# Turned queries read from PSUM, mLSTM heads at one step of the DeltaNet units, their loads and outputs issued by GpSimd, and earlier reads of the mLSTM output

## The chip, the cores and the metric

The kernel runs on one core of a Trainium2 chip. A core has TensorE (matrix products into PSUM), VectorE, ScalarE and GpSimd (elementwise work), SyncE (SP, which here only issues DMAs), and sixteen DMA engines that move data between the chip's memory and the on-chip memory SBUF. Each engine takes its instructions in order; semaphores order the engines among each other. DMAs are issued from the queues of SP, ScalarE and GpSimd.

The metric is the device time of one execution in microseconds (us). Lower is better.

## The reference

One decoder layer on 512 tokens of width 2048, with two token mixers side by side, an mLSTM with 8 heads (q and k of width 128, v of width 256) and a gated DeltaNet with 16 heads of width 128. Everything is float32.

```python
u = _rmsnorm(h, norm_w)
proj = jnp.matmul(u, w_in)            # q, k, v, o, z, gates of both mixers, two merge gates
h_a = _mlstm_chunkwise(heads(ml_q), heads(ml_k), heads(ml_v), i_pre, logf)   # q is scaled by dk ** -0.5
h_a = _merge_heads(_rmsnorm(h_a)) * ml_norm_w * sigmoid(ml_o) * silu(ml_z)
qkv = _causal_conv_silu(dn_qkv, dn_conv_w)
h_b = _gated_delta_chunkwise(l2norm(dq), l2norm(dk_), dv_, beta, g)
h_b = _merge_heads(_rmsnorm(h_b, dn_norm_w)) * silu(dn_z)
y = sigmoid(gate_a) * (h_a @ w_out[:ML_WIDTH]) + sigmoid(gate_b) * (h_b @ w_out[ML_WIDTH:])
out = _rmsnorm(x + y, final_norm_w)
```

In the mLSTM, q and k meet only in products of one with the other (the scores, and q times a state that is built of k and v). The factor dk ** -0.5 may therefore stand on either.

## The kernel before

Every large product is done in float32 accuracy out of three products of rounded parts: an operand x is cast to a high part `hi` and the rest `lo = x - hi`, and hi·hi, hi·lo and lo·hi are added up in PSUM. `split_hi` (L139, ScalarE) and `split_lo` (L142, VectorE) make the parts of the weights, some steps before TensorE needs them. `uh` and `ul` hold the parts of the activations.

The program runs in these stages:

1. Load and normalise x, turn it into `uh`, `ul`; project the first query and key heads.
2. `seven_stage`: the projections z, s, q, v and the merge gates. Each block multiplies two column groups c1 and c2 by a scheme of seven products for eight (`m6`, `m1`, `m5`, `m7`, sums in `U1` and `C22`). What ends a block is a "sink": it takes the results out of PSUM and writes them to memory. The q block (`sink_q`) takes the queries and keys of mLSTM heads 4 to 7. They are needed with the channel on the partitions: `V.transpose` turns blocks of 32x32, and four DMAs of 64 KB each (32 partitions, 16 blocks, runs of 128 bytes) put the blocks in place in `qt_d`; the keys are also written unturned to `k_d`.
3. `dn_unit`, eight units (L1105 and on). A unit projects K, V and Q of two DeltaNet heads (`proj_cm`, 16 steps each), and beside the matmuls the convolution, the norms, the solver of the delta rule and the chains of both heads run (`dn_front_k`, `dn_front_q`, `dn_back`, `dn_chain`). The eight mLSTM heads (`ml_head`) run beside the units too: loads of q, k, v, the scores `psc` (L1169), four chunks of products `pnum` and `pcs`, the gates `mg`, a turn, and the write to `hm_d`.
4. `load_h` reads `hm_d` back and splits it into `uh`, `ul` for the first part of the output projection (`wide_block`, three column blocks). Then `h_d`, the DeltaNet output, is read back, and `seven_stage` runs again with `w_out`.
5. `load_hm` reads `hm_d` a second time for the last column block (`last_block`), where the final norm and the output follow.

The order of the work: TensorE runs in the order in which the program is written. The program counts steps (`tick()`), one for every six matmuls or so; a generator that `start(gen, wait)` registers is continued at its due step, and `yield n` puts it off by n steps. A unit is 48 steps. The other engines' order is made by a planner that simulates the engines before the kernel is built: an instruction goes where it is ready, by priority. `urgent(...)` raises a priority, and `behind("A")`, `behind("V")`, `behind("S")` place an instruction right behind the newest weight cast of ScalarE, the newest weight difference of VectorE or the newest weight read of SP. On the chip the order of each queue is then fixed.

Tiles come from rings with a fixed number of buffers under a tag: "wr" has four, "tg" three, "to" two (turned tiles on their way out), "g" two (`gz` and `mg`); "mkq", "mkw", "mw" and "mv1" have one each (q and k, k turned back, decays, v). A buffer is free when all that reads it is done, a DMA included.

Lines that the prediction speaks of: L738 and L744, the turn and the four DMAs of `sink_q`; L853 and L863, the turn and the write of `turn`; L811, row broadcasts; L902, `pk`, the first product of a unit's solver, which needs the convolved key `kq` (L837); L1002, the first product of `dn_back`; L1082, the load of `gz`; L1098 and L1099, the norm factor of a chain's end and its product with `gz` on GpSimd; L1102, VectorE's product that waits for it; L1143, L1151, L1179 and L1213, the head's loads; L1157, the decays of a head; L1245 and L1246, the splits of `load_h` and `load_hm`; L1394, L1448 and L1565, other DMAs of GpSimd; L1520, the reads of `load_hm`.

Of the kernel before, what the change touches and what calls it, by code (L numbers as in the profile page):

```python
# [45 lines left out]

UNITS = list(range(8))
QKS = 2 * QKFIRST * P

# [8 lines left out]
def hybrid_body(  # L58
# [671 lines left out]
    def sink_q(c1, c2, m1, m5, m7, last):  # L730

        def turned(x_, c, a):
            if a:
                with behind("A"):
                    nc.scalar.dma_start(k_d[c], x_)
            o = spare(True)
            with behind("V"):
                V.transpose(o, x_)  # L738
            to = qt_d[a * 4:(a + 1) * 4].rearrange("h (j r) (n a c) -> r (h j) n a c", r=BS, n=NC, c=BS)
            ov = o.rearrange("p (m c) -> p m c", c=BS)  # L740
            for b in range(4):
                yield 1
                with behind("A"):
                    nc.scalar.dma_start(to[:, :, c, b, :], ov[b * BS:(b + 1) * BS])  # L744

        def out_(ps, t, a, wait):
            z = spare(False)
            with urgent(3):
                A.mul(z, ps, (float(P) ** -0.5, 1.0)[a])
            start(turned(z, t, a), wait + 6 * t)  # L750

        def end5(t):
            add(m5[t], U1[t], m5[t])
            out_(m5[t], t, 1, 8)

        def late_q(t):
            with behind("A"):
                A.mul(U1[t], U1[t], float(P) ** -0.5)
            yield from turned(U1[t], 2 + t, 0)

        def end7(t):
            add(U1[t], U1[t], m7[t])
            start(turned(C22[t], 2 + t, 1), 14 + 6 * t)
            start(late_q(t), 17 + 6 * t)

        return (lambda t: out_(m1[t], t, 0, 4)), end5, end7

# [80 lines left out]

    def turn(src, dst, out=False, lag=5):


        o = dst if dst is not src and len(dst.shape) == 3 else wk.tile([P, NC, P], F32, tag="to", name="to", bufs=2)
        V.transpose(o if len(src.shape) == 3 else o.rearrange("p n c -> p (n c)"), src)  # L853
        start(travel(o, dst, out, lag > 3), lag if out else 2)

    def travel(o, dst, out, apart):

        d = dst if len(dst.shape) == 4 else dr.tile([16, BS, 4, BS], F32, tag="td", name="td", bufs=8)
        ov = o.rearrange("p n (j c) -> p (n j) c", c=BS)
        if out:  # L860
            for a in range(4):
                with behind("A"):
                    nc.scalar.dma_start(d[:, :, a, :].rearrange("m r c -> r m c"), ov[a * BS:(a + 1) * BS])  # L863
# [178 lines left out]
    def dn_chain(j, hs, kq, u, soon):  # L1042
# [7 lines left out]
        for c in range(NC):  # L1050
# [29 lines left out]
            if c == 1:  # L1080
                g = wk.tile([P, NC, P], F32, tag="g", name="gz", bufs=2)
                nc.sync.dma_start(g, gz_d[:, :, h * P:(h + 1) * P].rearrange("c p n -> p c n"))  # L1082
            if c < NC - 1:
# [17 lines left out]
        with urgent():  # L1101
            V.tensor_tensor(out=g, in0=po, in1=g, op=ALU.mult)  # L1102
        turn(g, h_d[h], True, 5 if h < 2 * UNITS[-1] else 3)

# [33 lines left out]
    def ml_head(h):  # L1138
# [49 lines left out]
        for c in range(NC):  # L1188
# [20 lines left out]
            if c == NC - 2:  # L1209
                g = [wk.tile([P, NC, P], F32, tag="g", name="mg", bufs=2) for _ in range(2)]  # L1210
                for i in range(2):
                    col = h * NB + i * P
                    nc.sync.dma_start(g[i], g_d[:, :, col:col + P].rearrange("c p n -> p c n"))  # L1213
            yield 3
# [33 lines left out]
    def load_h():  # L1248

        raws_ = []  # L1250

        def load():
            if len(raws_) < KH:
                if len(raws_) % 2:
                    r = wkb.tile([P, NC, NB + 1], F32, tag="mv1", name="hr", bufs=1)
                    r = r.rearrange("p c n -> p (c n)")[:, 0:2 * S].rearrange("p (a s) -> p a s", s=S)
                else:
                    r = wkb.tile([P, 2, S], F32, tag="mkq", name="hr", bufs=1)
                for n in range(2):
                    load_tile(r[:, n, :], hm_d[2 * len(raws_) + n])  # L1260
# [12 lines left out]

    for h in range(MLH):
        start(ml_head(h), 1 + 42 * h, "B")
    start(open_y(), 200)
# [261 lines left out]
    def sink_last(c1, c2, m1, m5, m7):  # L1538
# [3 lines left out]
        def half_b():  # L1542
# [191 lines left out]
```

## Time and profile before

| | us |
|---|---|
| runs | 2216.82, 2210.53, 2212.88 |
| median | 2212.88 |
| profiled execution | 2213.26 |
| its span, first to last instruction | 2211.5 |
| mean granted clock of TensorE in it | 0.993 |

A profile is of one execution. Its lines name the engine (PE TensorE, PEld its weight loads, DVE VectorE, ACT ScalarE, POOL GpSimd, SP SyncE; a "q" behind it is the engine's queue, which issues DMAs and waits), the line of the kernel, and the tiles as out<-in. In a list of waits the figures are us in all, number of times, longest; the name behind the arrow is what ended the wait. In a view by stretches each row has start and end in us from the beginning of the span, then the busy time of each engine with its number of instructions, the granted clock of TensorE (1.00 is full speed), the busy share of the DMA engines, and GB/s. Matmuls overlap in the profile, so a busy TensorE isn't one at its peak.

### The profile page before, as it was taken

How to read it: one execution, taken by the hardware profiler on the slowest of the kernel's cores; microseconds unless marked ns; L12 is line 12 of the kernel's file. 1: busy time of each engine (PE TensorE's matmuls, PEld its weight loads, DVE VectorE, ACT ScalarE, POOL GpSimd, SP SyncE). 2: the span in 40 equal slices, each digit the busy share in tenths (PEclk: the TensorE clock that was granted, in tenths of full speed). 3: DMA queues.
4: the chain of work that ended last, by engine and by line, in shares of the span. 5: the costliest groups of instructions: out<-in, count | busy, mean ns of one | idle time of the engine just before them, and what ended most of it. 6: DMA issues, size and time to landing. Idle time of an engine off the chain costs nothing.

```text
span 2211.5 us, 31646 instructions
## 1 busy us (share of the span) xinstructions
PE 2146.4 (97%) x10544; PEld 1761.4 (80%) x10544; DVE 1698.6 (77%) x2937; ACT 1035.6 (47%) x1996; POOL 291.4 (13%) x395
## 2 busy tenths in 40 slices
PE   6999999999999999999999999999999999999997
PEld 5877777878887888888888888887877887877785
DVE  5787788788878777777857788778778776578886
ACT  5444444444444444444445545545445464344345
POOL 0320000000000000000012422324314121110200
PEclk9999999999999999999999999999999999999998
DMA  5456676667668757776867677768768577687886
GB/s 157 122 180 189 196 215 191 213 195 231 201 217 240 232 186 231 233 223 189 262 203 176 168 186 183 180 153 208 175 160 213 141 189 193 186 261 212 242 281 222
DMA packets 532006, 444.20 MB, mean 201 GB/s; under 512 B 250369, under 2 KB 385762, under 8 KB 531714
## 3 DMA queue, kind: packets, MB, share of 16 engines
q1 hardware_dynamic: 400946, 350.33, 55.2%
q10 hardware_dynamic: 124192, 74.02, 10.9%
q0 software_dynamic: 6704, 17.83, 3.6%
q8 instruction: 82, 1.34, 0.3%
q14 instruction: 82, 0.67, 0.1%
HBM read 348.66 MB, written 97.58 MB: 202 GB/s over the span
## 4 chain that ended last, share of the span: by engine, by line
PE 65%; DMA 14%; DVE 10%; issue 4%; ACT 2%; SPq 2%; POOL 1%; ACTq 0%; DVEq 0%; POOLq 0%
PE ps L577 11%; PE ps L578 11%; PE ps L576 10%; PE pj L256 8%; PE pj L257 8%; PE pj L258 8%; DVE wl L142 4%; DMA wr<-t_d 3%; DMA wr<-in_w_in_dram 2%; ACT wh L139 2%; DMA wr<-in_w_out_dram 1%; SPq L504 1%; DVE t L518 1%; DMA hr<-h_d 1%; PE py L1369 1%
## 5 line engine op out<-in xcount | busy, mean ns | idle before, releaser
L139 ACT CAST wh<-wr 128x512 fp32r<-128x512 f32 (+1 forms) x522 | 373.1, 717 | 388.8 <-PE pj L257 189.9
L142 DVE TENSOR_TENSOR wl<-wr,wh 128x512 fp32r<-128x512 f32 (+1 forms) x522 | 442.3, 850 | 144.1 <-ACT wh L139 137.1
L256 PE MATMUL pj<-uh,wh 128*128 128x512 f32 x896 | 373.6, 417 | 1.8 <-ACT yp L821 1.8
L258 PE MATMUL pj<-uh,wl 128*128 128x512 f32 x896 | 351.3, 392 | 0.0
L257 PE MATMUL pj<-ul,wh 128*128 128x512 f32 x896 | 350.9, 392 | 0.0
L577 PE MATMUL ps<-wl,uh 128*128 128x512 f32 x752 | 296.8, 395 | 5.7 <-DVE wl L142 5.1
L576 PE MATMUL ps<-wh,uh 128*128 128x512 f32 x752 | 294.7, 392 | 2.7 <-DVE X L630 2.4
L578 PE MATMUL ps<-wh,ul 128*128 128x512 f32 x752 | 294.0, 391 | 0.0
L139 ACT CAST wh<-ts 128x512 fp32r<-128x512 f32 x240 | 148.2, 617 | 256.4 <-DVE ts L536 209.6
L139 ACT CAST wh<-t 128x1024 fp32r<-128x1024 f32 x120 | 126.3, 1052 | 270.1 <-PE ps L578 144.1
L577 PE MATMUL ps<-wl,suh 128*128 128x512 f32 x624 | 243.1, 390 | 4.1 <-DVE wl L142 4.1
L576 PE MATMUL ps<-wh,suh 128*128 128x512 f32 x624 | 243.5, 390 | 1.0 <-ACT wh L139 0.5
L578 PE MATMUL ps<-wh,sul 128*128 128x512 f32 x624 | 242.9, 389 | 0.0
L258 PEld LDWEIGHTS pj<-uh,wl 128*128 128x128 f32 x896 | 168.7, 188 | 37.2
L256 PEld LDWEIGHTS pj<-uh,wh 128*128 128x128 f32 x896 | 169.5, 189 | 32.3 <-ACT yp L821 2.3
L257 PEld LDWEIGHTS pj<-ul,wh 128*128 128x128 f32 x896 | 169.6, 189 | 28.2
L142 DVE TENSOR_TENSOR wl<-ts,wh 128x512 fp32r<-128x512 f32 x240 | 164.4, 688 | 35.2 <-ACT wh L139 35.2
L142 DVE TENSOR_TENSOR wl<-t,wh 128x1024 fp32r<-128x1024 f32 x120 | 147.4, 1228 | 52.6 <-ACT wh L139 51.9
L577 PEld LDWEIGHTS ps<-wl,uh 128*128 128x128 f32 x752 | 141.8, 189 | 44.2 <-DVE wl L142 15.7
L576 PEld LDWEIGHTS ps<-wh,uh 128*128 128x128 f32 x752 | 141.7, 188 | 36.1 <-DVE X L630 6.3
L578 PEld LDWEIGHTS ps<-wh,ul 128*128 128x128 f32 x752 | 141.9, 189 | 28.7
L536 DVE TENSOR_TENSOR ts<-wr 128x512 f32<-128x512 f32 x120 | 82.8, 690 | 100.1 <-DMA wr<-t_d 77.8
(319 smaller groups left out, 3587.6 us busy)
## 6 DMA issues: line engine op xcount, KB each, us to landing
wr<-in_w_in_dram SPq DMA_DIRECT2D x744, 256.0 KB, 3.7
wr<-in_w_out_dram SPq DMA_DIRECT2D x138, 256.0 KB, 4.7
t_d<-ts ACTq DMA_DIRECT2D x104, 256.0 KB, 4.0
wr<-t_d SPq DMA_DIRECT2D x104, 256.0 KB, 3.9
xt<-in_x_dram SPq DMA_DIRECT2D x8, 512.0 KB, 7.4
tg_d<-X ACTq DMA_DIRECT2D x16, 256.0 KB, 5.6
tg_d<-to ACTq DMA_DIRECT2D x16, 256.0 KB, 6.0
v<-v_d SPq DMA_DIRECT2D x8, 512.0 KB, 5.2
```

The costliest lines, as they stand in the source:

```text
L139: newest["A"] = A.copy(hi, src).ins
L142: newest["V"] = V.tensor_tensor(out=lo, in0=src, in1=hi.bitcast(F32), op=ALU.subtract).ins
L256: T.matmul(ps[j], hi[:, k, wsl], uh[:, kt, :], start=(kt == 0), stop=False)
L257: T.matmul(ps[j], hi[:, k, wsl], ul[:, kt, :], start=False, stop=False)
L258: T.matmul(ps[j], lo[:, k, wsl], uh[:, kt, :], start=False, stop=(kt == KT - 1))
L504: newest["S"] = nc.sync.dma_start(to, src).ins
L518: V.tensor_tensor(out=t13, in0=r[:, 1:3, :], in1=r[:, 0:2, :], op=ALU.subtract)
L536: V.tensor_tensor(out=ts[:, 0, :], in0=r[:, 0, :], in1=r[:, 2, :], op=ALU.subtract)
L576: T.matmul(ps[t], ah, hi, start=(g == "A" and i == 0), stop=False, skip_group_check=True)
L577: T.matmul(ps[t], ah, lo, start=False, stop=False, skip_group_check=True)
L578: T.matmul(ps[t], al, hi, start=False, stop=(i == KH - 1), skip_group_check=True)
L1369: T.matmul(ps[c], uh[:, kt, tsl], hi, start=(kt == ks[0]), stop=False)
```

## The change

It has four parts.

- **Query block.** `end1` turns the first two query blocks straight from PSUM on VectorE. The scale is put on the keys instead of the queries (ScalarE, four times instead of six). The turned tiles come from "wr" instead of "tg", the 32 writes to `qt_d` are issued by GpSimd, two a step, and the waits of the pieces are set anew.
- **Heads.** The starts of the mLSTM heads are a list, `HEADS`, in place of 1 + 42h; from head 3 on they are 48 steps apart.
- **Issuers.** GpSimd issues the writes to `hm_d` (ScalarE before) and the loads of q, k, v, `mg` and of DeltaNet's `gz` (SP before).
- **Reading ahead.** `load_h` holds three pairs of tiles instead of two (the third in "mkw" and "mw"), and its splits are placed behind the weights'. `load_hm` reads four tiles ahead instead of two, into two rings, "hmr" and "hs", and starts two steps earlier.

```diff
+HEADS = (1, 41, 85, 130, 178, 226, 274, 322)
...
     def sink_q(c1, c2, m1, m5, m7, last):
 
-        def turned(x_, c, a):
+        def place(o, c, a):
+            to = qt_d[a * 4:(a + 1) * 4].rearrange("h (j r) (n a c) -> r (h j) n a c", r=BS, n=NC, c=BS)
+            ov = o.rearrange("p (m c) -> p m c", c=BS)
+            for b in range(4):
+                G.dma_start(to[:, :, c, b, :], ov[b * BS:(b + 1) * BS])
+                if b % 2:
+                    yield 1
+
+        def turned(x_, c, a, scale):
+            if scale:
+                with behind("A"):
+                    A.mul(x_, x_, float(P) ** -0.5)
             if a:
                 with behind("A"):
                     nc.scalar.dma_start(k_d[c], x_)
-            o = spare(True)
+            o = spare(False)
             with behind("V"):
                 V.transpose(o, x_)
...
+            yield 1
+            yield from place(o, c, a)
+
+        def end1(t):
+            o = spare(False)
+            with urgent(3):
+                V.transpose(o, m1[t])
+            start(place(o, t, 0), 2 + 3 * t)
...
         def end5(t):
             add(m5[t], U1[t], m5[t])
...
             z = spare(False)
             with urgent(3):
-                A.mul(z, ps, (float(P) ** -0.5, 1.0)[a])
-            start(turned(z, t, a), wait + 6 * t)
+                A.mul(z, m5[t], float(P) ** -0.5)
+            start(turned(z, t, 1, False), 10 + 4 * t)
...
         def end7(t):
             add(U1[t], U1[t], m7[t])
-            start(turned(C22[t], 2 + t, 1), 14 + 6 * t)
-            start(late_q(t), 17 + 6 * t)
+            start(turned(U1[t], 2 + t, 0, False), 16 + 3 * t)
+            start(turned(C22[t], 2 + t, 1, True), 22 + 4 * t)
...
-                nc.sync.dma_start(g, gz_d[:, :, h * P:(h + 1) * P].rearrange("c p n -> p c n"))
+                G.dma_start(g, gz_d[:, :, h * P:(h + 1) * P].rearrange("c p n -> p c n"))
...
-        turn(g, h_d[h], True, 5 if h < 2 * UNITS[-1] else 3)
+        turn(g, h_d[h], nc.scalar, 5 if h < 2 * UNITS[-1] else 3)
...
-            nc.sync.dma_start(kq[:, 1 - i, :], (qk_d if first else qt_d)[2 * QKFIRST * i + h % (2 * QKFIRST)])
+            G.dma_start(kq[:, 1 - i, :], (qk_d if first else qt_d)[2 * QKFIRST * i + h % (2 * QKFIRST)])
...
-            with behind("S"):
-                nc.sync.dma_start(kw, k_d[:, :, h * P - QKS:(h + 1) * P - QKS].rearrange("c p n -> p c n"))
+            with behind("V"):
+                G.dma_start(kw, k_d[:, :, h * P - QKS:(h + 1) * P - QKS].rearrange("c p n -> p c n"))
...
-        nc.sync.dma_start(v1[:, :, 0:NB], v_d[:, :, h * NB:(h + 1) * NB].rearrange("c p n -> p c n"))
+        G.dma_start(v1[:, :, 0:NB], v_d[:, :, h * NB:(h + 1) * NB].rearrange("c p n -> p c n"))
...
-                    nc.sync.dma_start(g[i], g_d[:, :, col:col + P].rearrange("c p n -> p c n"))
+                    G.dma_start(g[i], g_d[:, :, col:col + P].rearrange("c p n -> p c n"))
...
-            turn(g[i], hm_d[2 * h + i], True)
+            turn(g[i], hm_d[2 * h + i], G)
...
+                m = len(raws_) % 3
+                if m == 2:
...
+                elif m:
+                    r = [wkb.tile([P, NC, P], F32, tag=t, name="hr", bufs=1).rearrange("p c n -> p (c n)") for t in ("mkw", "mw")]
...
-        load()
-        load()
-        yield 4
+        for _ in range(3):
+            load()
+            yield 1
+        yield 1
...
-                split_scaled(uh[:, k, :], ul[:, k, :], raws_[i][:, n, :], normc[:, 16 + k:17 + k])
+                with behind("A"), behind("V"):
+                    split_scaled(uh[:, k, :], ul[:, k, :], raws_[i][n], normc[:, 16 + k:17 + k])
...
-        start(ml_head(h), 1 + 42 * h, "B")
+        start(ml_head(h), HEADS[h], "B")
...
-            r = fin["pool"].tile([P, NO], F32, tag="hmr", name="hmr", bufs=3)
+            if len(raws_) % 2:
+                r = late["sb"].tile([P, NO], F32, tag="hs", name="hmr", bufs=4)
+            else:
+                r = fin["pool"].tile([P, NO], F32, tag="hmr", name="hmr", bufs=3)
...
-        for _ in range(2):
-            load(nc.sync)
-        yield 4
+        for _ in range(4):
+            with behind("S"):
+                load(nc.sync)
+            yield 1
...
-            start(load_hm(), 5)
+            start(load_hm(), 3)
```

More of the change, by code (lines that the diff above doesn't have):

```diff
@@ L735, in turned, with end5 @@
                     nc.scalar.dma_start(k_d[c], x_)
-            o = spare(True)
+            o = spare(False)
             with behind("V"):
                 V.transpose(o, x_)
[L739 to L746, printed above, removed]
+            yield 1
[5 more added lines that the diff above has]
+            start(place(o, t, 0), 2 + 3 * t)
+        def end5(t):
+            add(m5[t], U1[t], m5[t])
             z = spare(False)
             with urgent(3):
-                A.mul(z, ps, (float(P) ** -0.5, 1.0)[a])
-            start(turned(z, t, a), wait + 6 * t)
[L752 to L759, printed above, removed]
+                A.mul(z, m5[t], float(P) ** -0.5)
+            start(turned(z, t, 1, False), 10 + 4 * t)
         def end7(t):
             add(U1[t], U1[t], m7[t])
-            start(turned(C22[t], 2 + t, 1), 14 + 6 * t)
-            start(late_q(t), 17 + 6 * t)
-        return (lambda t: out_(m1[t], t, 0, 4)), end5, end7
+            start(turned(U1[t], 2 + t, 0, False), 16 + 3 * t)
+            start(turned(C22[t], 2 + t, 1, True), 22 + 4 * t)
+        return end1, end5, end7
     SINK = {"q": sink_q, "g": sink_flat(lambda c, col: tg_d[c, :, col - GATE:col - GATE + NO], AF.Tanh, 0.5),
@@ L847, in token_norms, with turn @@
                 A.activation(jk, pk[:, c, :], AF.Square, accum_out=dst[:, c:c + 1])
-    def turn(src, dst, out=False, lag=5):
+    def turn(src, dst, out=None, lag=5):
         o = dst if dst is not src and len(dst.shape) == 3 else wk.tile([P, NC, P], F32, tag="to", name="to", bufs=2)
@@ L861, in travel @@
             for a in range(4):
-                with behind("A"):
-                    nc.scalar.dma_start(d[:, :, a, :].rearrange("m r c -> r m c"), ov[a * BS:(a + 1) * BS])
+                with behind("A") if out is nc.scalar else ExitStack():
+                    out.dma_start(d[:, :, a, :].rearrange("m r c -> r m c"), ov[a * BS:(a + 1) * BS])
                 if apart:
@@ L1253, in load @@
             if len(raws_) < KH:
-                if len(raws_) % 2:
+                m = len(raws_) % 3
+                if m == 2:
                     r = wkb.tile([P, NC, NB + 1], F32, tag="mv1", name="hr", bufs=1)
                     r = r.rearrange("p c n -> p (c n)")[:, 0:2 * S].rearrange("p (a s) -> p a s", s=S)
+                    r = [r[:, n, :] for n in range(2)]
+                elif m:
+                    r = [wkb.tile([P, NC, P], F32, tag=t, name="hr", bufs=1).rearrange("p c n -> p (c n)") for t in ("mkw", "mw")]
                 else:
                     r = wkb.tile([P, 2, S], F32, tag="mkq", name="hr", bufs=1)
+                    r = [r[:, n, :] for n in range(2)]
                 for n in range(2):
-                    load_tile(r[:, n, :], hm_d[2 * len(raws_) + n])
+                    load_tile(r[n], hm_d[2 * len(raws_) + n])
                 raws_.append(r)
-        load()
-        load()
-        yield 4
+        for _ in range(3):
+            load()
+            yield 1
+        yield 1
         for i in range(KH):
```

## The prediction, made before the changed kernel had run

> **What bounds the kernel now.** The first view is part 1 of the page, the busy time of each engine.
>
> ```profile
> PE 2146.4 (97%) x10544; PEld 1761.4 (80%) x10544; DVE 1698.6 (77%) x2937; ACT 1035.6 (47%) x1996; POOL 291.4 (13%) x395
> ```
>
> TensorE is occupied for 2146.4 of 2211.5 us, and the change removes no matmul. So whatever it wins must come out of the 65 us in which TensorE stood still, or out of time in which it ran at a lower granted clock. The second view is the list of waits of TensorE (time in all, times, longest).
>
> ```profile
> PE ps L577 <- DVE wl L142: 9.7, 12, 2.4
> PE pk L902 <- DVE kq L837: 8.6, 4, 5.4
> ...
> PE pj L256 <- ACT yp L821: 1.8, 1, 1.8
> ...
> PE pw L1064 <- DVE r L1059: 1.4, 1, 1.4
> PE pr L1056 <- DVE st L1077: 1.4, 1, 1.4
> PE pst L1071 <- ACT w L1067: 1.2, 2, 1.0
> ```
>
> Apart from the start of the kernel, which the change leaves alone, the waits are few and short, and on VectorE or ScalarE being late. Where they lie shows in the third view, the busy time by stretch (start:end, length, then PE, PEld, DVE, ACT, POOL, and after them granted clock, DMA share, GB/s). The first three rows are the stretches around the query block, the loads of the mLSTM output and the last block; the next four are DeltaNet units 3 to 6, each from its first K matmul to that of the next unit.
>
> ```profile
> 698.00:712.00 14.00, 11.40 (x43) 8.68 (x42) 10.43 (x14) 5.11 (x9) 0.00 (x0) 0.88 1.00 267
> 1820.00:1840.00 20.00, 16.05 (x80) 12.41 (x79) 13.94 (x40) 10.47 (x20) 0.00 (x0) 1.00 0.74 202
> 2166.00:2192.00 26.00, 22.03 (x84) 15.89 (x83) 17.43 (x27) 16.08 (x37) 0.57 (x1) 0.93 0.49 157
> ...
> 1382.70:1470.70 88.00, 87.77 (x534) 73.08 (x532) 68.45 (x180) 47.49 (x131) 29.50 (x37) 1.00 0.74 178
> 1470.70:1561.20 90.50, 88.68 (x537) 74.18 (x537) 70.52 (x179) 46.95 (x131) 27.53 (x37) 1.00 0.74 179
> 1561.20:1658.30 97.10, 91.61 (x541) 76.76 (x540) 70.18 (x179) 47.66 (x130) 27.90 (x39) 0.96 0.69 170
> 1658.30:1748.70 90.40, 87.18 (x531) 72.64 (x530) 70.67 (x179) 45.52 (x128) 31.81 (x41) 1.00 0.74 183
> ```
>
> A stall costs twice: as a gap, and as the lower clock that may follow it. Both are taken from these rows, as length minus PE busy and as length times (1 minus clock).
>
> **The change part by part.** The sum is made against the profiled execution, 2213.26 us (span 2211.5 and 1.8 around it); the median of the runs, 2212.88, lies 0.4 below it and is not corrected for.
>
> *The query block.* Its stretch holds a gap of 14.00 - 11.40 = 2.6 us and 0.12 x 14 = 1.7 us of lost clock, 4.3 in all. These rows say why (waits from 666 to 712 us; then the issues of that DMA: shortest, median, longest in ns):
>
> ```profile
> ACT wh L139 <- DMA qt_d<-to: 11.3, 4, 4.5
> ...
> PE ps L577 <- DVE wl L142: 2.4, 1, 2.4
> ```
>
> ```profile
> L744 ACTq DMA_DIRECT2D qt_d<-to x32: 309/458/1631, 672.7 to 714.1; - x32
> ```
>
> ScalarE takes its queue in order, so the 32 writes of turned queries and keys held up the casts of the weights (L139) behind them for 11.3 us; the low halves (L142) came late, and TensorE waited 2.4 us. The change issues all 32 from GpSimd, which does nothing in this stretch (POOL 0.00). It also takes the turned tile out of the three buffers "tg", which the weight sums `ts` use too, and puts it in "wr". Transposes stay eight; two of them now read PSUM and run ahead of the weights:
>
> ```profile
> L738 DVE STREAM_TRANSPOSE to<-X x4: 705/710/712, 692.8 to 708.2; 128x512 f32<-128x512 f32 x4
> ```
>
> No row shows one that reads PSUM; I take the 0.7 us of this row, for two, and cost it at nothing because ScalarE loses two scalings of the same shape in exchange. If that cover is gone, it is 1.4 us once. What is late next is GpSimd. Its price for an issue:
>
> ```profile
> L811 POOL DMA_DIRECT2D gb<-rows_d x16: 536/618/627, 1150.4 to 1768.3; - x16
> ```
>
> ```profile
> L1448 POOL DMA_DIRECT2D ty<-tg_d x12: 546/577/587, 1973.8 to 2100.7; - x12
> ```
>
> ```profile
> L1565 POOL DMA_DIRECT2D ty<-tg_d x1: 727/727/727, 2109.1 to 2109.1; - x1
> ```
>
> The first two describe 128 runs of memory, the third 256. A write of turned data is 512 runs of 128 bytes, and no row shows GpSimd issuing that. From one side, 150 ns for 128 more runs gives 577 + 3 x 150 = 1.03 us; from the other, strictly by the number of runs, 4 x 0.6 = 2.4 us. I take 1.03, because the 256-run row already falsifies proportion. Then 32 issues take 33 us. The code spreads them over 26 steps of six matmuls, and matmuls start 0.22 to 0.23 us apart (TensorE's timeline: start, duration):
>
> ```profile
> 1603.33 0.39 PE L257 MATMUL pj<-ul,wh 128*128 128x512 f32 x1
> 1603.55 0.40 PE L258 MATMUL pj<-uh,wl 128*128 128x512 f32 x1
> 1603.78 1.05 PE L1169 MATMUL psc<-mkq 128*128 128x128 f32 x8
> ```
>
> So a step is 1.4 us and the 26 are 36 us: it fits, barely. Term: **-4**.
>
> *The heads.* Unit 3 is undisturbed at 88.0 us; units 4 to 6 take 90.5, 97.1 and 90.4, so 2.5, 9.1 and 2.4 over. The code gives the reason for the last two. A unit has 48 steps; `psc` comes 12 steps after a head's start, the unit's `pk` at steps 24 and 25. Heads at 42h start at steps 1, 43, 37, 31, 25, 19, 13 and 7 of their units, so the psc of heads 6 and 7 falls at 25 and 19, on or just before pk. TensorE's timeline shows it: in unit 5 the psc at 1603.78, quoted above, and then these; in unit 6 the last two.
>
> ```profile
> 1604.77 0.69 PE L1002 MATMUL p<-tn,aq 32*32 32x32 f32 x32
> 1610.83 1.41 PE L902 MATMUL pk<-kq 128*128 128x128 f32 x5 [5.37 <-DVE kq L837]
> ...
> 1691.34 1.06 PE L1169 MATMUL psc<-mkq 128*128 128x128 f32 x8
> ...
> 1700.59 1.13 PE L902 MATMUL pk<-kq 128*128 128x128 f32 x8 [1.38 <-DVE kq L837]
> ```
>
> The new starts put heads 3 to 7 all at step 34: psc at 46, the chunks at 9 to 21 of the next unit, clear of pk and near head 3's place (31), whose neighbourhood had no stall. I count units 5 and 6, 9.1 + 2.4, and leave unit 4's 2.5, where psc was not near. Term: **-11**.
>
> *Loads and outputs of the heads by GpSimd.* These loads leave SP, where they stood in front of weight reads while waiting for buffers (waits of SP's queue from 1100 to 2000 us), and go where these two waits are (whole run):
>
> ```profile
> SPq L1213 <- DVE to L853: 16.5, 9, 3.5
> ...
> SPq L1082 <- DVE to L853: 5.4, 5, 2.2
> ```
>
> ```profile
> POOL wm L1157 <- PE pnum L1190: 85.5, 5, 39.6
> ```
>
> ```profile
> DVE gz L1102 <- POOL gz L1099: 7.0, 5, 3.0
> ```
>
> No wait of TensorE is traced to SP, so the relief there is worth nothing by itself. On GpSimd a head and its unit add 8 writes of `hm_d`, 2 gate loads each for `mg` and `gz`, v and (from head 4) k, 14 issues at 1.03, and two of q and k at 0.6: 15.6 us beside the 28 to 32 that the unit rows show, so 47 of 88. Throughput is no matter; order is. A load that waits for a "g" buffer now blocks `dm` (L880), `rsd` and `gz` (L1098, L1099) behind it, VectorE waits for gz at L1102, and its queue holds the weights' low halves. The price lies between -2.5 (unit 4's excess, the only one not counted yet) and, if each of 16 chain ends stands behind two issues and a third of it reaches TensorE, 16 x 2.06 / 3 = 11. I take **+3**, near the 7.0 us that VectorE waits there already, of which most stays hidden.
>
> By the Trainium skill, page "DMA: Bandwidth & Descriptors", section "Issuing engines are not separate DMA queues", DMAs from any queue share the same 16 engines, and another issuer saves only the issue time. By that rule this part and the query part would bring almost nothing; the 1.00 DMA share at 698 to 712 agrees with it, the 11.3 us of in-order waits on ScalarE speak against it.
>
> *Reading further ahead.* In the loads of the mLSTM output (waits from 1800 to 1890 us) and in the last block (2108 to 2192 us):
>
> ```profile
> ACT uh L1245 <- DMA hr<-hm_d: 12.2, 7, 3.8
> ```
>
> ```profile
> ACT uh L1245 <- DMA hmr<-hm_d: 6.5, 3, 4.6
> ```
>
> ```profile
> PE py L1369 <- ACT uh L1245: 1.5, 1, 1.5
> PE py L1369 <- ACT wh L139: 1.1, 1, 1.1
> PE py L1371 <- DVE ul L1246: 1.0, 2, 0.7
> ```
>
> `load_h` gets a third pair of buffers and its splits go behind the weights'; the gap it caused is 20.00 - 16.05 = 3.95 us. The last head now ends 27 steps later, inside the last unit, beside these splits; so I take **-3**. `load_hm` reads four ahead instead of two, into seven buffers instead of three; its stretch has a gap of 3.97 us and 0.07 x 26 = 1.8 of lost clock. I take **-5** of 5.8. What is late next there are the weights themselves, at the 1.1 us row.
>
> Sum: -4 - 11 + 3 - 3 - 5 = -20, so 2213.3 - 20 = **2193 us**.
>
> **The rivals.** *Everything goes:* unit 4's 2.5 and the rests of the terms (0.3, 0.5, 1.0, 0.8) vanish as well and GpSimd costs nothing: 2193 - 5 - 3 = 2185. *The stall moves to the last unit:* head 7's products and writes meet load_h and the last chains; load_h's 3 are not won and one stall like that at 1604 (5.4 us) appears: 2193 + 3 + 5.4 = 2201. For it: DVE is at 70 of 88 to 97 us in every unit. *The DMA engines are the bound:* the query and head parts bring nothing, as the same bytes move; left are -3 - 5 + 3, so 2208, no measurable change. For it the DMA share of 1.00 at 698; against it 0.69 in unit 5, the worst one. *GpSimd becomes the bound (slower):* an issue of 512 runs costs 2.4 us. Then a unit has 14 x 2.4 + 1.2 + 28 = 63 of 88 us, the four `hm_d` writes ahead of a chain end hold VectorE 9.6 us, and four units instead of one lose unit 5's 9.1 us; the query writes need 77 us instead of 36 and their stall stays. 2213.3 + 3 x 9.1 - 8 = 2233. The query block suffers from 1.1 us an issue (36 / 32); the units from 2 us, where four writes outlast the three weight parts that are prepared ahead, 3 x 2 steps x 1.4 = 8 us, and that is where it decides.
>
> The Trainium skill, page "SBUF — State Buffer", section "Who interferes with whom", has a mechanism for this rival: VectorE's two-port copies and tensor_scalars lock GpSimd out while it writes descriptors. The L811 row disagrees so far: its 16 issues beside a VectorE about 80% busy stay within 536 to 627 ns.
>
> **How the numbers follow.** Forecast 0.46, everything goes 0.15, last unit 0.17, DMA bound 0.13, GpSimd bound 0.09. A difference under 0.3% (6.6 us) is about what cannot be told from no change here. The first three lie below 2206: 0.78 faster; the fourth within: 0.13; the last: 0.09 slower. The range runs from a little under "everything goes", 2182, to past the DMA case, 2209; 0.09 lies above it, and some of the edges.
>
> **What would show it.** Right: no PE wait on kq at L902 over 1 us, units 4 to 7 alike near 88 us, no ScalarE wait on qt_d, hr or hmr, a full clock around 705, 1610 and 2187, and GpSimd issues of qt_d and hm_d near 1 us. Wrong: such issues above 2 us, new waits of VectorE at L1102 on gz or at L853 on hm_d writes, or the stall of 1604 back in the last unit.

## The result, and the profile after

| | before | after |
|---|---|---|
| median of six runs each, us | 2213.31 (2210.53 to 2223.08) | 2192.39 (2189.28 to 2196.02) |
| profiled execution, us | 2213.26 | 2194.43 |
| its span, us | 2211.5 | 2192.6 |

The ratio is 0.9898, with a 95% interval of 0.9877 to 0.992: about 22 us faster, 0.6 us from the forecast of 2193. The lines of the changed kernel lie 1 to 17 further down: the casts are L140 and L143, `kq` L843, the turn L859, `pk` L908, the write of `hm_d` L869 and of `td` L875. First the busy times of the page, as they were read before.

```profile
PE 2141.9 (98%) x10544; PEld 1757.7 (80%) x10544; DVE 1713.2 (78%) x2937; ACT 1036.4 (47%) x1994; POOL 392.6 (18%) x551
```

GpSimd carries 101 us more than the 291.4 of before. TensorE's occupied time fell by only 4.5 us; the rest of the 18.9 us of span came out of its gaps. The list of TensorE's waits says which (in all, times, longest):

```profile
PE ps L578 <- DVE wl L143: 10.6, 15, 2.4
PE pw L1070 <- DVE r L1065: 3.6, 1, 3.6
```

`pk <- kq`, 8.6 us before, is gone, and so are the waits of the output's products on `uh` and `ul`. A new one of 3.6 us stands in front of `pw`. To place gain and loss, both kernels are cut at the same five points of the program: the start of the first `seven_stage`, of unit 0, of the output's first part, of the second `seven_stage`, of the last block, and the end (view by stretches, columns as in the prediction). The kernel before:

```profile
124.70:1138.90 1014.20, 1003.12 (x4370) 817.72 (x4370) 806.86 (x1017) 457.46 (x659) 8.11 (x17) 1.00 0.68 212
1138.90:1832.20 693.30, 680.93 (x4003) 568.50 (x4001) 531.62 (x1332) 359.23 (x943) 209.11 (x284) 1.00 0.74 181
1832.20:1989.10 156.90, 151.46 (x801) 124.15 (x800) 105.42 (x209) 64.73 (x146) 24.07 (x28) 0.99 0.74 210
1989.10:2149.80 160.70, 155.90 (x673) 126.85 (x672) 130.50 (x172) 68.02 (x96) 17.05 (x23) 0.99 0.82 245
2149.80:2211.50 61.70, 47.16 (x193) 36.38 (x191) 41.34 (x70) 29.07 (x60) 2.59 (x4) 0.91 0.62 226
```

The changed kernel:

```profile
125.10:1140.70 1015.60, 1004.41 (x4369) 815.72 (x4368) 806.34 (x1017) 456.59 (x657) 31.09 (x52) 1.00 0.68 212
1140.70:1822.90 682.20, 678.57 (x4003) 568.13 (x4002) 548.75 (x1350) 359.64 (x942) 286.80 (x403) 1.00 0.73 183
1822.90:1973.60 150.70, 149.20 (x801) 123.23 (x800) 103.60 (x192) 66.04 (x148) 25.20 (x30) 1.00 0.80 223
1973.60:2137.00 163.40, 157.25 (x673) 126.56 (x673) 131.74 (x175) 67.81 (x96) 16.93 (x23) 0.99 0.82 245
2137.00:2192.60 55.60, 44.11 (x193) 35.78 (x191) 39.84 (x68) 29.23 (x60) 2.59 (x4) 0.92 0.65 238
```

The units give 11.1 us, the output's first part 6.2, the last block 6.1. The two `seven_stage`s are 1.4 and 2.7 us longer; the second is not touched by any part and lay between 158.4 and 163.6 us in all the runs below, so these two differences are not read. The query block lies in the first of them; what it won there is looked at where it was changed alone. Inside the units (the same view; units 1 and 3 to 7 of the changed kernel):

```profile
1213.20:1302.00 88.80, 85.18 (x504) 70.84 (x502) 71.23 (x181) 44.23 (x111) 36.00 (x55) 0.98 0.71 178
...
1389.60:1476.40 86.80, 86.80 (x531) 72.78 (x530) 73.30 (x178) 46.15 (x126) 38.28 (x54) 1.00 0.70 172
1476.40:1563.10 86.70, 86.70 (x530) 72.76 (x529) 71.64 (x177) 46.07 (x126) 38.14 (x54) 1.00 0.76 189
1563.10:1650.00 86.90, 86.90 (x532) 72.90 (x530) 72.17 (x177) 46.18 (x126) 38.30 (x54) 1.00 0.75 191
1650.00:1736.70 86.70, 86.70 (x530) 72.76 (x530) 71.62 (x176) 46.05 (x126) 37.97 (x53) 1.00 0.73 183
1736.70:1822.90 86.20, 86.19 (x523) 71.84 (x522) 71.03 (x177) 48.87 (x128) 31.56 (x42) 1.00 0.73 179
```

Units 3 to 7 have no gap any more; 97.1 us has become 86.9. Unit 1, which took 83.4 us before, takes 88.8, with a gap of 88.80 - 85.18 = 3.6 us and 0.02 x 88.8 = 1.8 us of lost clock. What happens there is in the timelines of four engines (start, duration; in brackets the idle time before, and what ended it). VectorE:

```profile
1282.76 0.19 DVE L954 TENSOR_TENSOR xi<-xi,tmp 128x28 f32<-128x28 f32 x1
1288.73 0.71 DVE L859 STREAM_TRANSPOSE to<-mg 128x512 f32<-128x512 f32 x1 [5.78 <-DMA td<-to]
...
1289.46 0.34 DVE L1065 SCALAR_TENSOR_TENSOR r<-pr,negeg,vt 128x128 f32<-128x128 f32 x1
```

GpSimd:

```profile
1278.71 2.67 POOL L869 DMA_DIRECT2D hm_d<-to  x4 [5.98 <-DVE to L859]
1281.43 0.79 POOL L1088 DMA_DIRECT2D gz<-gz_d  x1
...
1282.26 0.76 POOL L1185 DMA_DIRECT2D v<-v_d  x1
```

SP:

```profile
1279.74 2.53 SPq L875 DMA_DIRECT2D td<-to  x4
```

TensorE:

```profile
1289.86 0.79 PE L1070 MATMUL pw<-r,tb 128*128 128x128 f32 x2 [3.62 <-DVE r L1065]
```

The ring "to" has two buffers. One holds a turned `mg` whose four `hm_d` writes GpSimd issues, the other a turned `vt` whose four `td` writes SP issues up to 1282.3. The next turn needs one of them. The last `hm_d` write lands at 1284.9, the last `td` write, issued at 1281.3, only at 1288.6, and by the trace it is this one that ends the wait. In between GpSimd has sent the loads of `gz` and of v, 256 and 512 KB. VectorE stands 5.78 us in front of a turn that nobody is in a hurry for, with `r`, which TensorE needs, behind it in its queue.

### The profile page after: what moved, and what is told of

Read it like the earlier page. It is cut to its first block, busy times and chain, and to the rows that moved or that the text cites. A ratio compares the mean times of both kernels' runs of the same rounds, so it can differ in the third digit from the quotient of the medians.

```text
span 2192.6 us, 31712 instructions
## 1 busy us (share of the span) xinstructions
PE 2141.9 (98%) x10544; PEld 1757.7 (80%) x10544; DVE 1713.2 (78%) x2937; ACT 1036.4 (47%) x1994; POOL 392.6 (18%) x551
## 4 chain that ended last, share of the span: by engine, by line
PE 72%; DMA 12%; DVE 8%; issue 4%; ACT 2%; SPq 1%; POOL 0%; ACTq 0%; DVEq 0%; POOLq 0%
PE ps L578 11%; PE ps L577 11%; PE ps L579 11%; PE pj L257 9%; PE pj L259 9%; PE pj L258 9%; DVE wl L143 4%; DMA wr<-t_d 3%; DMA wr<-in_w_in_dram 3%; PE py L1382 1%; PE py L1384 1%; PE py L1383 1%; ACT wh L140 1%; DMA wr<-in_w_out_dram 1%; SPq L505 1%
## 5 line engine op out<-in xcount | busy, mean ns | idle before, releaser
L140 ACT CAST wh<-wr 128x512 fp32r<-128x512 f32 (+1 forms) x522 | 373.2, 716 | 405.8 <-PE pj L258 240.1
L143 DVE TENSOR_TENSOR wl<-wr,wh 128x512 fp32r<-128x512 f32 (+1 forms) x522 | 440.9, 848 | 110.9 <-ACT wh L140 101.8
L140 ACT CAST wh<-ts 128x512 fp32r<-128x512 f32 x240 | 148.0, 617 | 260.4 <-DVE ts L537 203.0
L140 ACT CAST wh<-t 128x1024 fp32r<-128x1024 f32 x120 | 126.3, 1053 | 271.9 <-PE ps L579 153.9
L143 DVE TENSOR_TENSOR wl<-ts,wh 128x512 fp32r<-128x512 f32 x240 | 164.2, 687 | 34.4 <-ACT wh L140 34.4
L143 DVE TENSOR_TENSOR wl<-t,wh 128x1024 fp32r<-128x1024 f32 x120 | 146.8, 1223 | 53.2 <-ACT wh L140 52.6
```

The source lines that it names most:

```text
L140: newest["A"] = A.copy(hi, src).ins
L143: newest["V"] = V.tensor_tensor(out=lo, in0=src, in1=hi.bitcast(F32), op=ALU.subtract).ins
```

## The experiments

All kernels compute the whole of the reference. A median is given with its range and its ratio to the kernel before in the same rounds.

### Each part alone

`q_only`, `heads_only`, `issuers_only` and `ahead_only` are the kernel before with one part of the change each.

```diff
q_only:        + the new sink_q
heads_only:    + HEADS = (1, 41, 85, 130, 178, 226, 274, 322)
issuers_only:  + G.dma_start for kq, kw, v1, mg, gz and for the writes of hm_d
ahead_only:    + the new load_h and load_hm, start(load_hm(), 3)
```

> The kernel before with the query part alone. In-order queue theory (the prediction): the waits of ScalarE on qt_d go, the stall at 701 us and its lost clock go, total 4 us less than before, 2209. Rival (DMA engines full in that stretch): the stall stays where it is, total within 1 us of before. From the trace of the changed kernel, where a new wait of 1.5 us stands at 745 us, about 2 us less is also possible; then a VectorE that runs late is the remaining cause.

> The kernel before with the new starts of the heads alone. Collision theory (the prediction): the stall of TensorE at pk in unit 5 and that in unit 6 go, units 3 to 6 last 87 to 88 us each, total 9 to 14 us less. Rival (the issuers did it: waiting DMAs on ScalarE's and SP's queues were the cause): the stalls stay or move, total at most 4 us less.

> The kernel before with the heads' loads and outputs on GpSimd alone. The prediction: nothing gained, 0 to 6 us more (3 taken), the stall at pk in unit 5 stays. Rival (the waiting DMAs were the cause): units 4 to 6 lose their stalls, 8 us or more less. GpSimd issues of 512 runs take 0.65 to 0.8 us as in the trace of the changed kernel.

> The kernel before with the earlier reads of the mLSTM output alone. The prediction: 8 us less (3 at the first read, 5 in the last block), the waits on hr and hmr gone. The trace of the changed kernel shows 6 less in the first part of the output projection and 7 less in the last block; if these come from this part alone, 12 to 13 less. Rival (the first 6 came from the heads' new places): 6 to 8 less, and the wait on hr stays.

| | median (range) | ratio, 95% | us from before |
|---|---|---|---|
| q_only | 2208.35 (2205.92 to 2216.87) | 0.9969 (0.9949 to 0.9988) | -6.9 |
| heads_only | 2201.83 (2200.74 to 2207.38) | 0.9942 (0.9921 to 0.9963) | -12.8 |
| issuers_only | 2216.81 (2208.59 to 2225.69) | 1.0009 (0.9986 to 1.0032) | +2.0 |
| ahead_only | 2205.28 (2204.18 to 2210.44) | 0.9955 (0.9937 to 0.9972) | -10.0 |

The last column is the ratio less 1, times 2213.3. Three parts win, the issuers do not. The sum is -27.7, the whole change gave -21 to -23 (and -20 by the ratio of a second measurement, `after_again` below): some 5 to 8 us less. The four intervals together are wider than that (about 9 us either way, added in squares), so the times alone would not prove a loss; the trace has one of about 5 us, the stall of unit 1. It is in none of the four: unit 1 takes 83.5, 83.5, 83.7 and 83.5 us there, by the same view.

### The whole change less one thing

Three kernels are the changed kernel with the loads back on SP, with the outputs back on ScalarE, and with head 1 at another step.

```diff
after_loads_sp:  - G.dma_start(kq, v1, g, gz, kw)   + nc.sync.dma_start(...)
after_outs_act:  - turn(g[i], hm_d[2 * h + i], G)   + turn(g[i], hm_d[2 * h + i], nc.scalar)
head1_36:        - HEADS = (1, 41, 85, ...)         + HEADS = (1, 36, 82, ...)
```

> The changed kernel with the heads' loads (q, k, v, mg and gz) issued by SP again, the outputs still by GpSimd. Prediction's view: the loads' issuer is worth nothing or costs up to 3 us, so 2189 to 2193. A theory for the new stall at 1286 us in unit 1: two loads of GpSimd (gz and v) are issued in the middle of the turned tiles' writes and slow them; then the stall goes and unit 1 lasts 84 us instead of 89, total 2187. Rival: the loads on GpSimd free SP for weight reads and bring something; then above 2196.

> The changed kernel with the writes of hm_d issued by ScalarE again, the loads still by GpSimd. If the new stall at 1286 us comes from outputs by GpSimd that hold the two turned tiles, it goes and unit 1 lasts 84 us, total 2187. If it comes from the loads, it stays, 2192. Rival (in-order queue theory as in the query block): ScalarE's casts are held up by the writes, units 2 to 7 get 1 us longer each, total 2198.

> The changed kernel with heads 1 and 2 at steps 36 and 82 instead of 41 and 85, so that all heads from the second stand at steps 34 to 36 of a unit. If the stall at 1286 us is a meeting of head 1's turned outputs (steps 35 and 39 of unit 1) with the turned values of the unit (36 and 39), it goes: unit 1 at 84 us, total 2187. If it is the issuer alone, it stays: 2192.

Measured: 2187.91 (2186.24 to 2194.7), 0.9891 (0.9862 to 0.992); 2192.16 (2188.94 to 2195.8), 0.9905 (0.9877 to 0.9932); 2191.41 (2186.79 to 2196.24), 0.9894 (0.9863 to 0.9925). By these ratios none of the three can be told from the changed kernel (0.9898), and the totals expected for a stall that goes, 2187, were met by the first alone; what follows is read from the traces. Unit 1 (view by stretches) of `after_loads_sp`:

```profile
1214.80:1298.50 83.70, 83.70 (x504) 69.67 (x502) 70.36 (x180) 44.11 (x111) 31.99 (x47) 1.00 0.76 190
```

Of `after_outs_act`:

```profile
1211.70:1295.20 83.50, 83.50 (x503) 69.80 (x502) 70.10 (x177) 43.94 (x111) 28.07 (x42) 1.00 0.74 181
```

Of `head1_36`:

```profile
1216.20:1301.30 85.10, 84.10 (x504) 69.71 (x503) 74.81 (x182) 41.65 (x105) 36.56 (x54) 1.00 0.74 193
```

And the turn that waited 5.78 us, in VectorE's timeline of `after_loads_sp`:

```profile
1286.59 0.71 DVE L859 STREAM_TRANSPOSE to<-mg 128x512 f32<-128x512 f32 x1 [2.09 <-DMA td<-to]
```

In these runs the stall is there in full only with all three: the loads on GpSimd, the outputs on GpSimd, and head 1 at that step (with heads 1 and 2 moved no turn waits for a `td` write; the 1.0 us of gap that is left is at two other waits of 0.5 us). With the loads on SP, v is issued at 1285.1, behind the `td` writes and one more weight read; the same turn waits 2.09 us instead of 5.78, and none of it reaches TensorE. That the loads slow the `td` writes on the DMA engines is the plain reading: the last of them takes 7.3 us to land in the changed kernel, 3.8 here. It is not shown. No run moved the v load alone, and in `after_q_act` (below), where `gz` and v go out behind the `td` writes just as in the changed kernel, the last write lands in 4.2 us and the gap is 0.8 us. So in these runs the three conditions are needed, but they don't suffice.

Beside loads on GpSimd, the outputs on GpSimd earn their place. With them on ScalarE units 4 to 6 take 88.1, 88.4 and 88.3 us, 1.5 more than the 86.7 to 86.9 of the changed kernel, and TensorE waits for ScalarE's copies `w` of a chain (units 4 to 6):

```profile
PE pst L1077 <- ACT w L1073: 3.0, 3, 1.3
```

So `after_outs_act` loses there what it saves in unit 1, and its units have the 682.2 us of the changed kernel, while those of `after_loads_sp` have 676.9. But `heads_only`, with the outputs on ScalarE and the loads on SP, has 86.8, 86.8 and 86.7 us in units 4 to 6 and no wait of TensorE there: with the loads on SP, the outputs on ScalarE cost these units nothing. The changed kernel with loads and outputs both put back, that is, without the issuers' part, was not run.

### Which end of a head makes the stall

The prediction blamed `psc`, 12 steps after a head's start, on steps 24 and 25 of a unit. In the kernel before, the end of the preceding head (its two products with `mg` and two turns, 42 steps after its start) also moves: it falls at steps 25, 19, 13 and 7 of units 3 to 6. In the changed kernel it falls at step 28 of units 3 to 7, just past `pk`. Two kernels take these apart. `heads_on_pk` puts psc on step 25 of units 2 to 5, with ends at step 7; `heads_end13` puts ends at step 13 of units 3 to 5, with psc at 31.

```diff
heads_on_pk:  + HEADS = (1, 43, 109, 157, 205, 253, 295, 334)
heads_end13:  + HEADS = (1, 43, 115, 163, 211, 259, 301, 334)
```

> The changed kernel with heads 2 to 5 at step 13 of units 2 to 5, so that their scores fall on step 25, where pk is, as head 6 did in the kernel before; heads 1, 6 and 7 at 43, 295 and 334. Collision theory: each of units 2 to 5 grows from 87 to between 90 and 97 us, total 12 to 40 us more than the changed kernel. Rival (the stall in unit 5 was an accident of late transfers, not of the step): units 2 to 5 stay within 1.5 us of 87, total within 5 us of the changed kernel.

> The changed kernel with heads 2 to 5 at step 19 of units 2 to 5 (starts 115, 163, 211, 259; the others at 1, 43, 301, 334). Their scores fall on step 31, well past pk, but the end of each, the gate products and the turned outputs (42 steps after the start), on step 13 of the next unit, ahead of pk, as that of head 5 did in unit 5 of the kernel before. End theory: units 3 to 5 grow from 87 to between 90 and 97 us each. Scores theory (the prediction's): units 3 to 5 stay within 1.5 us of 87.

Measured: 2201.32 (2197.33 to 2206.36), 0.9943 (0.9922 to 0.9964); and 2217.8 (2215.22 to 2224.67), 1.0021 (1.0006 to 1.0036). Units 2 to 6 of `heads_on_pk` (view by stretches):

```profile
1293.80:1380.50 86.70, 86.70 (x531) 72.87 (x530) 70.11 (x182) 46.15 (x124) 23.61 (x34) 1.00 0.62 151
1380.50:1468.80 88.30, 86.67 (x532) 72.98 (x530) 71.28 (x178) 46.16 (x126) 39.02 (x55) 1.00 0.72 175
1468.80:1557.90 89.10, 87.39 (x531) 72.65 (x530) 74.74 (x177) 45.59 (x126) 39.91 (x55) 1.00 0.74 185
1557.90:1647.30 89.40, 87.43 (x532) 72.63 (x530) 74.52 (x177) 45.80 (x126) 39.19 (x55) 1.00 0.76 184
1647.30:1733.90 86.60, 86.60 (x531) 72.80 (x530) 73.04 (x177) 45.54 (x128) 46.64 (x63) 1.00 0.76 194
```

Units 2 to 6 of `heads_end13`:

```profile
1298.00:1382.50 84.50, 84.50 (x522) 70.99 (x520) 71.38 (x179) 44.26 (x120) 24.47 (x35) 1.00 0.64 156
1382.50:1474.90 92.40, 88.52 (x531) 73.94 (x530) 69.55 (x178) 45.88 (x126) 38.18 (x53) 0.98 0.68 164
1474.90:1566.10 91.20, 88.37 (x531) 73.65 (x529) 71.95 (x177) 45.87 (x126) 38.65 (x54) 0.98 0.74 181
1566.10:1656.90 90.80, 86.99 (x532) 72.69 (x530) 70.95 (x177) 45.94 (x126) 38.76 (x54) 1.00 0.72 182
1656.90:1752.50 95.60, 90.70 (x542) 76.13 (x540) 69.61 (x179) 47.77 (x130) 39.79 (x58) 0.98 0.68 173
```

In unit 2 of `heads_on_pk` psc falls on step 25 with no end near it: no gap at all. With an end at step 7 as well there is a gap of 1.6 to 2.0 us a unit, at `pk` in unit 3, in units 4 and 5 mostly at a chain's `pr`; that is less than the collision theory expected and more than its rival. In `heads_end13` an end at step 13 costs 3.9, 2.8 and 3.8 us in gaps, all of them at `pk <- kq`, and up to 1.8 in clock, with psc six steps past `pk`. Its unit 2 has the same head start and the same psc, but no end ahead of `pk`: no gap. Unit 6, an end at 13 and psc at 25, as in unit 5 of the kernel before, comes to 95.6 us, beside 97.1 there (with 542 and 541 matmuls, against 531 to 537 in the units beside them). So the head's end makes the stall by itself, and psc adds to it where an end is near. In all, `heads_end13` is 23 us slower than the changed kernel in the same rounds (2194.41, below), by its starts alone; by the view its units 3 to 6 take 370.0 us instead of 347.1. VectorE's timeline of the kernel before, ahead of the 5.37 us wait, shows how it works (the view lists no idle time between these rows):

```profile
1599.40 0.68 DVE L1228 TENSOR_TENSOR mg<-v,mg 128x512 f32<-128x512 f32 x1
...
1601.27 0.69 DVE L853 STREAM_TRANSPOSE to<-mg 128x512 f32<-128x512 f32 x1
...
1604.88 0.69 DVE L1228 TENSOR_TENSOR mg<-v,mg 128x512 f32<-128x512 f32 x1
...
1606.17 0.70 DVE L853 STREAM_TRANSPOSE to<-mg 128x512 f32<-128x512 f32 x1
...
1609.41 0.68 DVE L1171 TENSOR_TENSOR wm<-psc,wm 128x512 f32<-128x512 f32 x1
1610.01 0.68 DVE L837 SCALAR_TENSOR_TENSOR kq<-th,kq 128x512 f32<-128x512 f32 x1
```

`kq`, for which TensorE waits, stands behind four instructions of the head's end, 2.8 us, and one of psc, 0.7. That is this one stall. Ahead of the 2.8 us wait in unit 4 of `heads_end13` only one of the four stands, 0.88 us, behind a weight difference of 2.44 us, which takes 0.68 as a rule. VectorE's timeline:

```profile
1512.67 2.44 DVE L143 TENSOR_TENSOR wl<-wr,wh 128x512 fp32r<-128x512 f32 x1
...
1516.02 0.88 DVE L1234 TENSOR_TENSOR mg<-v,mg 128x512 f32<-128x512 f32 x1
```

GpSimd's timeline, beside it:

```profile
1513.50 1.05 POOL L1230 TENSOR_TENSOR mg<-mg,sm 128x512 f32<-128x512 f32 x1
```

This product on GpSimd belongs to the head's end too. In unit 5 of `heads_end13` the same 2.44 us stand at the same place. So the end of a head makes VectorE late in two ways, by its own work there and, as far as these rows show, by slowing what VectorE does beside GpSimd's product.

### Who issues the writes of the query block

`after_q_act` is the changed kernel with the 32 writes of `qt_d` back on ScalarE; ring, spacing and the turns from PSUM stay. `loads_sp_again` repeats `after_loads_sp`, and `after_again` is the changed kernel, all in the same rounds.

```diff
after_q_act:  -                G.dma_start(to[:, :, c, b, :], ov[b * BS:(b + 1) * BS])
              +                with behind("A"):
              +                    nc.scalar.dma_start(to[:, :, c, b, :], ov[b * BS:(b + 1) * BS])
```

> The changed kernel with the 32 writes of qt_d issued by ScalarE again, all else of the query part kept. In-order queue theory: ScalarE's casts wait on these writes again, the stall near 701 us and its lost clock come back, 3 to 4 us more than the changed kernel, 2196. Rival (the ring of the turned tiles was the cause, which is still the new one): no stall there, within 1 us of the changed kernel.

> The changed kernel with the heads' loads issued by SP again, once more and in more rounds. If the loads by GpSimd cost only the stall at 1286 us, it is 4 to 5 us faster than the changed kernel beside it, 2188. If the earlier difference was between chips, within 1.5 us of it.

> The changed kernel itself, on the same chip and in the same rounds: 2192, with the stall of TensorE near 1286 us in unit 1 (3.6 us and its lost clock), as the profile of the first run has it.

Measured: 2191.96 (2187.22 to 2195.5), 0.9898 (0.9876 to 0.992); 2189.3 (2185.08 to 2191.72), 0.9882 (0.9861 to 0.9903); 2194.41 (2187.54 to 2198.51), 0.991 (0.989 to 0.9929). The stretch from 698 to 712 us in `after_q_act`:

```profile
698.00:712.00 14.00, 14.00 (x64) 11.58 (x62) 12.34 (x17) 5.75 (x9) 0.00 (x0) 1.00 1.05 283
```

ScalarE's wait for the writes, in the list of waits from 666 to 712 us:

```profile
ACT wh L140 <- DMA qt_d<-to: 3.3, 1, 3.3
```

No gap, full clock, with ScalarE as the issuer. Its waits for the writes are 6.8 us in all instead of 11.3: the 3.3 of this row, and 3.5 just behind the window, at 713. In the kernel before, four writes in a row took 4.24 us ahead of one cast (at 692.7). Here half of the writes go out in ones and twos; of the four bunches of four, those at 698.4 and 703.9 took 2.2 us each with no cast waiting for them, and the 3.5 us behind the last held up no matmul. So it was not the engine. Which of the ring, the spacing and the turns from PSUM did it was not taken apart.

`loads_sp_again` has 677.0 us in its units, as `after_loads_sp` had; `after_again` has 682.1, with a wait of 2.9 us at the same `pw`. In the same rounds it is 5.1 us by the medians. The intervals of the two ratios overlap, but both pairs of traces show 5 us in the units, 5.1 of it in unit 1 in the first pair and 3.4 in the second. `after_q_act`, also with the loads on GpSimd, has 678.0. So the loads on GpSimd cost 1 to 5 us, with the size of the stall. The changed kernel with the loads left on SP is the best version that was run, by its medians and by the time in its units.

## Why the prediction was right, and where it was not

The total was right, in part by luck: several steps were off and made up for one another.

- **The query block, -4.** The gap at 701 us and its lost clock went, as said; the stretch with the block after it fell by 3.0 us in `q_only` (672 matmuls from 596.7 us on, from 158.0 to 155.0 by TensorE's timeline). The time of `q_only` fell by 6.9; the rest is not traced to this part, and its units are 3.5 us shorter in the profile, though nothing in them was changed. In the whole first `seven_stage` the 3 us are no more than its spread: 1012.2 to 1018.2 us in the ten kernels with the new block, 1014.2 to 1020.6 in the four with the old. The part's reason, the issuer, fell with `after_q_act`. By the Trainium skill, page "DMA: Bandwidth & Descriptors", section "Issuing engines are not separate DMA queues", another issuer saves only the issue time: with 2191.96 against 2194.41 us this case agrees for these writes. For the heads' loads the issuer was worth more than the issue, 5.1 us by the medians of those rounds. The price of a GpSimd issue was too high: 0.65 us, not 1.03 (the `qt_d` writes of after, ns):

```profile
L737 POOL DMA_DIRECT2D qt_d<-to x32: 648/651/838, 669.0 to 710.6; - x32
```

- **The heads, -11.** -12.8 by the ratio, -13.0 in the units of `heads_only` (680.4 us). The size was near, by offsets: units 3 to 6 of `heads_only` won 18.9 us together (86.8, 86.8, 86.8 and 86.7 us), and the last unit, into which the last head moved, lost 5.7 (89.2 us, 20 matmuls more and a gap of 2.6). The cause was not right: the step that failed is "psc on or just before pk". The bulk of it was the other burst of the same heads, their end, which the new starts put just past `pk`. It fits that unit 4's 2.5 us, left out because psc was not near, went too: a head ended at its step 19. And of the 3.2 us of gap in unit 6 only 1.4 stood at `pk`; 1.8 stood at `pj <- yp`, a row that the prediction shows, where TensorE waited for ScalarE.
- **The issuers, +3.** +2.0 alone, with zero inside the interval. Inside the whole change the loads cost 1 to 5 us. The prediction looked for it at `gz`; VectorE's waits there did grow, from 7.0 to 9.6 us, but they are 16.1 in `heads_only`, where SP issues the load, and no wait of TensorE is traced to them. The price was paid at a two-buffer ring, by a turn that waits for a DMA. No term of the prediction has it; its signs of being wrong name a wait at that line, but on `hm_d` writes, and it came on `td` writes. Beside the loads on GpSimd, the outputs off ScalarE save 1.5 us in each of three units.
- **Reading ahead, -3 and -5.** -5.7 in the output's first part and -5.0 in the last block of `ahead_only` (151.20 and 56.70 us by the same cuts), -6.2 and -6.1 in the first pair of profiles. Over all traces the terms are smaller: by the same cuts the output's first part takes 150.7 to 155.7 us, 153.0 on the mean, in the ten kernels that read ahead, and 157.0 on the mean in the four others; the last block takes 56.0 and 61.3. So -4 and -5 are nearer, and the prediction was close. ScalarE's wait on `hr <- hm_d`, 12.2 us, is gone; that on `hmr` fell from 6.5 to 2.6, and a new one of 1.7 stands at a weight cast. The last head beside these splits leaves a gap of 0.01 us in unit 7, but the unit is longer by what moved into it, 86.2 us instead of 83.5.
- **The rivals.** Of "everything goes", the stalls of units 3 to 7 did go, and 2185 is near what the version with the loads on SP reaches (2187.91 and 2189.3). "GpSimd becomes the bound" needed issues of 2 us; they take 0.65 to 0.79. "The stall moves" was right in kind and wrong in place: to unit 1, not to the last; in `heads_only`, without the earlier reads, the last unit does have a gap, of 2.6 us, where the kernel before has 1.6.

Still open: why the stall of unit 1 varies (gaps of 3.6 and 2.9 us in two profiles of the changed kernel, 0.8 in `after_q_act`; the last `td` write lands in 7.3, 6.3 and 4.2 us), and why unit 6 of the kernel before had a gap of 3.2 us with an end at step 7 and psc at 19, where `heads_on_pk`, with the same steps and the rest of the change, has none.

## What to carry to other kernels

When a critical instruction waits on an in-order engine, list what that engine did just before it, and ask of each burst of the neighbouring work, its beginning and its end, where it falls; moving one task by some steps can then be worth more than making anything cheaper. Test a bundled change part by part, and test the whole less one part too, since a loss can need several parts together. Where a ring of two buffers is emptied by DMAs, look for their landing: here a late one held VectorE, which issues no DMA, for 5.78 us.

## What the runs showed of the hardware

- A GpSimd issue of 512 runs took 0.65 us for the writes from 32 partitions (row above) and 0.78 us for the load of `gz` to 128 partitions, against 0.56 us for q and k with 128 runs. Four times the runs cost 0.1 to 0.2 us. The issues of `gz` (ns, as above):

```profile
L1088 POOL DMA_DIRECT2D gz<-gz_d x16: 765/782/815, 1281.4 to 1851.5; - x16
```

The loads of q and k in the same view:

```profile
L1149 POOL DMA_DIRECT2D mkq<-qt_d x8: 552/562/569, 1428.7 to 1690.1; - x8
```

- VectorE turns a 128x512 tile out of PSUM as fast as out of SBUF: 712 ns here, 704 where the same kernel turns `X` (L750).

```profile
L757 DVE STREAM_TRANSPOSE to<-ps x2: 707/712/717, 668.0 to 669.7; 128x512 f32<-128x512 f32 x2
```

- After the stall in unit 1 TensorE's granted clock stood at half for 3.4 us, as after that of 2.4 us at 701 us in the kernel before. The stretch in the changed kernel:

```profile
1289.36:1292.78 3.42, 2.92 (x8) 2.44 (x9) 3.35 (x12) 0.27 (x1) 3.04 (x5) 0.50 0.73 176
```

But a gap of 3.0 us at 701.7 us in `ahead_only` was followed by full clock:

```profile
701.70:710.00 8.30, 5.29 (x24) 4.34 (x24) 6.60 (x10) 3.03 (x5) 0.00 (x0) 1.00 0.94 233
```

The Trainium skill, page "TensorE: Matmul & The Clock Gate", section "What's actually happening", has a free-running window of about 3.4 us that decides on the clock. The traces agree, and show its phase. In each of the fourteen, all changes of the granted clock lie on one grid of 3.413 us (in the kernel before at 704.75, 708.16, 1609.28, 1882.34, 2066.66 and 2186.13 us, among others). The gap of 2.4 us lies in one cell of this grid with 2.3 us, the 3.6 us of unit 1 with 3.1; the 3.0 us of `ahead_only` are split into 1.6 and 1.4, and the 2.9 us of `after_again`, also followed by full clock, into 1.03 and 1.87. Counted over all traces from 130 to 2170 us, every cell at full clock in which TensorE stood still for more than 1.9 us was followed by half clock, none with less than 1.35 was, and between the two some were.

- VectorE's weight difference (128x512, both operands in SBUF) slows down beside operations of GpSimd on two tensors. In `heads_end13` the 286 of 404 that have nothing of GpSimd beside them take 0.64 to 0.70 us; 32 take over 1 us, up to 3.07, and each of these has such an operation of GpSimd beside it. Issues of DMAs by GpSimd alone don't do it: 0.64 to 0.69 us in 37 cases.
